# A sixth Strassen group in the input projection, and a branch's product moved into the attention loop

## The chip, the cores and the metric

The kernel runs on one core of one Trainium2 chip. A core has a matrix engine (TensorE, "PE" in the profile; its weight loads are shown as "PEld"), a vector engine (VectorE, "DVE"), an engine for activations and copies (ScalarE, "ACT"), a general engine (GpSimd, "POOL") and a queue engine (SyncE, "SP"). Each engine works through its own list of instructions in order, and waits for the others by semaphores. SP and POOL also issue the transfers between the chip's memory (DRAM) and the on-chip buffers. [...] The metric is the device time of one execution in microseconds (us); less is better.

## The reference

One layer of an encoder trunk over 1024 tokens of width 1024, in 32-bit numbers:

```python
h = x + 1/2 * SwiGLU_1(RMSNorm(x))
u = RMSNorm(h)
[qA|kA|vA|qB|kB|vB|gA|gB] = u @ W_in
yA = NeighbourhoodAttention2D(qA, kA, vA)       # 8 heads of 64, learned 2-D bias
yB = WindowedGQA(rope(qB), rope(kB), vB)        # 8 heads of 64 over 2 key heads, sink logit per head
h = h + (sigmoid(gA) * (yA @ W_A) + sigmoid(gB) * (yB @ W_B)) @ W_out
h = h + 1/2 * SwiGLU_2(RMSNorm(h))              # inner width 2816
y = RMSNorm_final(h)
```

W_in has 512 columns each for qA, kA, vA and qB, 128 each for kB and vB, and 1024 each for the gates gA and gB: 34 chunks of 128 columns, of which chunks 18 to 25 are gA and 26 to 33 are gB.

## The kernel before

Precision: every 32-bit factor is split into a high part (a cast on ACT) and the rest (a subtraction, mostly on DVE), and a product is made of three matmuls, high x high, high x low, low x high (mm3, lines 142 to 149). A plain product of one 128-column chunk with all 1024 tokens takes 8 blocks of the inner width x 2 halves of the tokens x 3 matmuls of 128x512.

Strassen: the two feed-forward stages, most of W_in and W_out are done in Strassen's scheme with seven products in place of eight. For W_in the list "groups" (line 875) names the chunks: a group is two pairs of chunks, and is worked as 7 products x 2 pairs x 4 blocks x 3 matmuls. The results are recombined as they leave PSUM (store_z, from line 879) and stored to DRAM: the first part of attention A's operands as high and low parts, the rest as z_d, and gate chunks to g_d. Chunks which are in no group are the list "gates" (line 877).

The attention loop (lines 1338 to 1362) then runs over 64 units: 32 of branch B (units_b, line 1223) and 32 of branch A (units_a, line 1242). A unit is one tile of 128 tokens and two heads. In iteration n the loop issues

- scores of unit n (line 1268): four matmuls into two PSUM banks of tag "d", on DVE the sum with the bias and the row's minimum, on ACT the exponential with its sum, on DVE the reciprocal, and the scaling of the two heads, one on DVE (line 1290) and one on ACT (line 1291);
- half of the iteration's share of filler steps;
- turn of unit n-1 (line 1293): up to six transposes into two more "d" banks, each split into high and low part by ACT and DVE;
- the other half of the filler;
- values of unit n-2 (line 1306) into a bank of tag "g", and the unit's write, which adds high and low parts on DVE.

There are four banks of tag "d" and four of tag "g". Branch B's write collects four units for a store to y_d, branch A's writes go to a part of the tile fa and are stored to y_d by halves; both stores are issued by POOL. Operands of attention A are fetched ahead by prep_a (line 1077). The bias of a head pair is fetched and added to the mask by load_bias when its first unit is made.

The filler (line 1199) is a generator of short pieces of matrix work, six matmuls a step: first the gates, eight steps a chunk, with the next chunk's weights loaded and split in between; then branch_b (line 1182), which multiplies branch B's attention output with W_B, four steps for each of eight chunks, applies the gate as the bank is read, and leaves the result in the tiles "merged"; at last six steps of branch A's product with W_A. How many filler steps an iteration takes is set by "rate" (line 1322); what is left is drained after the loop (line 1363). The gate's sigmoid is applied on ACT to the gate that is fetched back from g_d (gate_b, line 1176; a_prep, line 1390).

After the loop come the last W_B steps, the product with W_A (lines 1406 to 1424), whose operand is split from y_d by split_y, the merge with W_out (Down, line 1387), and the second feed-forward stage.

The order of instructions on each engine is the program's order as a planner sees it: the framework ranks the instructions by their place in the program, plays the engines through with assumed costs, takes the next one that is ready, and assigns free buffers and banks as it goes. Buffers are named by tags: raw (4), xs (2), ws (8), hs (6).

Of the kernel before, what the change touches and what calls it, by code (L numbers as in the profile page):

```python
# [15 lines left out]
P = 128  # L16
# [6 lines left out]
HD = 64  # L23
# [13 lines left out]
def trunk_kernel(ctx, tc, x, xt, n1, wg1, wu1, wd1, nm, win, rpb, sink, wa, wb, wo,  # L37
# [837 lines left out]
    groups = [[(12, 13), (14, 15)], [(16, 17), (0, 1)], [(4, 5), (8, 9)], [(2, 3), (6, 7)], [(10, 11), (18, 19)]]  # L875
# [192 lines left out]

    def load_bias(s, h):
        braw = raw4()[:, :384]  # L1070
        nc.sync.dma_start(braw, bias_d[h])
# [104 lines left out]
    def gate_b(dc):  # L1176
        rb = xs4()
        nc.sync.dma_start(rb, g_d[D + dc * P:D + (dc + 1) * P, :])
        nc.scalar.activation(rb, rb, AF.Sigmoid)
        return rb  # L1180

    def branch_b():

        for c in range(2, 4):
            split_y(Y_B[c], c * P, nc.vector if c == 2 else nc.gpsimd)
        for g in (4, 6):
            new_ar(g, F32)
        nxt = branch_w(wb[0], 0, nc.vector), gate_b(0)
        for dc in range(NC8):
            w, rb = nxt  # L1190
            bs = [bank("dg"[dc % 2]) for _ in range(2)]
            yield from branch_mm(bs, w, Y_B)
            if dc + 1 < NC8:
                nxt = branch_w(wb[0], dc + 1, nc.vector), gate_b(dc + 1)
            for n in range(2):
                sl = slice(n * 512, (n + 1) * 512)
                nc.vector.tensor_tensor(merged(dc)[:, sl], bs[n], rb[:, sl], op=ALU.mult)

    def filler():
        for dc, nxt in zip(gates, gates[1:] + [None]):  # L1200
            if nxt is not None:
                yield from gate(dc, {4: lambda: mix.update(gate=load_w(win[0], GA + nxt * P))})
            else:
                yield from gate(dc, {0: lambda: [fetch_y(c * P) for c in range(2)],
                                     4: lambda: [split_y(Y_B[c], c * P, nc.gpsimd) for c in range(2)],
# [12 lines left out]
    def small(name, n=2):  # L1218
        return main.tile([P, 2], F32, tag=name, bufs=n, name=nm_(name))

    ybox = {}

    def units_b():
        for j in range(NTT):
            for c in range(4):
                def write(o, j=j, c=c):

                    if c == 0:
                        ybox["b"] = xs4()[:, :512].rearrange("p (c t) -> p c t", c=4)
# [12 lines left out]
    def units_a():  # L1242
        for hp in range(4):
# [3 lines left out]
            for j in range(NTT):  # L1247
                def write(o, j=j, hp=hp):

                    y = fa[:, 3072:4096]  # L1250
# [3 lines left out]
                    for s in range(2):  # L1254
                        rows = slice(s * HD, s * HD + HD)
                        nc.vector.tensor_tensor(y[rows, j * P:(j + 1) * P], o[:HD, s, 0, :], lo[:, s, :], op=ALU.add)
                    if j in (3, 7) and hp < 3:
                        cols = slice((j - 3) * P, (j + 1) * P)
                        nc.gpsimd.dma_start(y_d[512 + hp * P:512 + (hp + 1) * P, cols], y[:, cols])
# [8 lines left out]
    def scores(un):  # L1268
# [7 lines left out]
        for s in range(2):  # L1276
# [3 lines left out]
            pr = fa[:, 1536 + (2 * (npair[0] % 2) + s) * (384 + ext):][:, :ext + nw]  # L1280
            if ext:
                nc.vector.tensor_copy(pr[:, 0:1], un["sink"][s])
# [8 lines left out]
        nc.scalar.activation(un["pr"][1], un["pr"][1], AF.Copy, scale=rc[:, 1:2])  # L1291
# [30 lines left out]
    rate = (nfill - 44) / 64.0  # L1322
# [15 lines left out]
    for n in range(1 << 30):  # L1338
# [218 lines left out]
```

## Time and profile before

| | |
|---|---|
| median of 3 runs | 1935.32 us (1935.28 to 1936.85) |
| profiled execution: span from the first to the last instruction | 1934.8 us; the page gives no other time of that execution |
| mean granted TensorE clock | 0.998 of full |
| TensorE busy | 1922.2 us, 99% |
| VectorE busy | 1437.1 us, 74% |
| ScalarE busy | 943.6 us, 49% |
| GpSimd busy | 295.5 us, 15% |
| projection W_in: first and last result copied from a bank by ACT (line 911) | 647.7 to 842.7 us of the span |
| attention loop (first and last score matmul) | 841.7 to 1114.7 us |
| branch B's product (its gate multiplications) | 1132.8 to 1169.4 us |
| branch A's gate multiplications | 1179.5 to 1212.9 us |

How to read the views. The page begins with each engine's busy time and its number of instructions; then the span is cut in 40 slices, with one digit of busy share, in tenths, for each. The chain of work that ended last is followed back from the last instruction and summed by engine and line. A row of groups reads: line, engine, operation, output<-inputs by the program's names, shapes, xcount | busy us, mean ns of one | idle time of the engine just before them, and what ended it. A row of the table by stretches reads: from:to, then time (length), and for PE, PEld, DVE, ACT and POOL the busy us and the number of instructions, the granted clock, the share of the transfer engines and GB/s. A row of the timeline reads: start us, length us, engine, line, operation. Matmuls are pipelined, so lengths of neighbours overlap; the distance of their starts tells their price.

### The profile page before, as it was taken

The page shows a single profiled execution, that of the slowest core. Times are in us where ns is not written, and L with a number is a line of the kernel's source. Part 1 is how long each engine was busy: PE and PEld are TensorE (multiplying, and loading weights), DVE is VectorE, ACT ScalarE, POOL GpSimd, SP SyncE. Part 2 cuts the span into 40 slices and gives each one's busy share as a digit, 9 for nine tenths or more (in the row PEclk, how much of TensorE's full clock was granted, in tenths as well). Part 3 has the DMA queues.
Part 4 walks back from the last instruction along what each step waited for, and adds up shares of the span by engine and source line. Part 5 has one row for each costly group of instructions (what it writes and reads, how often), then busy time and mean ns, then how long its engine had stood idle before and what let it go on. Part 6 is the DMA issues. An engine that isn't in the chain of part 4 may idle for free.

```text
span 1934.8 us, 25499 instructions
## 1 busy us (share of the span) xinstructions
PE 1922.2 (99%) x8956; PEld 1603.1 (83%) x8956; DVE 1437.1 (74%) x2560; ACT 943.6 (49%) x1827; POOL 295.5 (15%) x432
## 2 busy tenths in 40 slices
PE   9999999999999999999999999999999999999998
PEld 7888888888888888888888888878888888888886
DVE  7987765668957788678888857889676566569864
ACT  6532333344446543477877862365333333344453
POOL 0011110013300112211122231010111001005210
PEclk9999999999999999999999999999999999999999
DMA  6344323286234478553458576533423323493341
GB/s 261 100 167 163 129 104 128 86 289 225 88 109 137 159 223 250 185 163 104 116 134 195 184 242 210 169 140 133 147 87 109 126 87 109 140 355 104 112 144 61
DMA packets 151745, 298.70 MB, mean 154 GB/s; under 512 B 14912, under 2 KB 64448, under 8 KB 151616
## 3 DMA queue, kind: packets, MB, share of 16 engines
q1 hardware_dynamic: 123072, 210.53, 33.6%
q0 software_dynamic: 27824, 85.48, 13.3%
q8 instruction: 71, 1.16, 0.3%
q10 hardware_dynamic: 720, 1.05, 0.1%
q14 instruction: 58, 0.48, 0.1%
HBM read 210.50 MB, written 88.27 MB: 154 GB/s over the span
## 4 chain that ended last, share of the span: by engine, by line
PE 88%; issue 7%; POOL 1%; DMA 1%; DVE 1%; ACT 1%; POOLq 0%; SPq 0%; ACTq 0%; DVEq 0%
PE g L149 16%; PE g L147 16%; PE g L145 16%; PE d L149 11%; PE d L147 11%; PE d L145 11%; PE d L1299 2%; PE g L1313 1%; PE g L1318 1%; PE d L1278 1%; PE d L1279 1%; POOL zs_d L889 1%; PE d L138 1%; POOL z_d L891 1%; DMA zr_d<-xs 0%
## 5 line engine op out<-in xcount | busy, mean ns | idle before, releaser
L145 PE MATMUL g<-ar,ws 128*128 128x512 f32 x1128 | 423.1, 395 | 0.6 <-ACT fa L911 0.6
L147 PE MATMUL g<-ar,ws 128*128 128x512 f32 x1128 | 417.2, 390 | 0.9 <-DVE ar L94 0.5
L149 PE MATMUL g<-ar,ws 128*128 128x512 f32 x1128 | 416.1, 390 | 0.2 <-DVE ws L311 0.2
L145 PE MATMUL d<-ar,ws 128*128 128x512 f32 x736 | 282.4, 391 | 0.3 <-ACT ar L810 0.2
L147 PE MATMUL d<-ar,ws 128*128 128x512 f32 x736 | 281.9, 390 | 0.3 <-DVE ar L812 0.3
L149 PE MATMUL d<-ar,ws 128*128 128x512 f32 x736 | 281.6, 390 | 0.5 <-DVE ws L311 0.5
L147 PEld LDWEIGHTS g<-ar,ws 128*128 128x128 f32 x1128 | 211.8, 188 | 46.2 <-DVE ar L94 1.0
L149 PEld LDWEIGHTS g<-ar,ws 128*128 128x128 f32 x1128 | 211.7, 188 | 45.5 <-DVE ws L311 0.7
L145 PEld LDWEIGHTS g<-ar,ws 128*128 128x128 f32 x1128 | 206.4, 188 | 37.8 <-ACT fa L911 1.0
L311 DVE TENSOR_TENSOR ws<-raw,ws 128x512 fp32r<-128x512 f32 x204 | 139.6, 690 | 99.6 <-ACT ws L308 98.8
L308 ACT CAST ws<-raw 128x512 fp32r<-128x512 f32 x204 | 125.1, 620 | 140.6 <-PE g L149 64.4
L145 PEld LDWEIGHTS d<-ar,ws 128*128 128x128 f32 x736 | 138.3, 188 | 29.7 <-ACT ar L810 0.6
L147 PEld LDWEIGHTS d<-ar,ws 128*128 128x128 f32 x736 | 138.4, 188 | 29.6 <-DVE ar L812 0.6
L149 PEld LDWEIGHTS d<-ar,ws 128*128 128x128 f32 x736 | 138.4, 188 | 29.4 <-DVE ws L311 0.7
L93 ACT CAST ws<-raw 128x512 fp32r<-128x512 f32 (+1 forms) x121 | 81.0, 669 | 144.0 <-PE d L149 61.8
L94 DVE TENSOR_TENSOR ws<-raw,ws 128x512 fp32r<-128x512 f32 (+1 forms) x119 | 93.7, 789 | 59.8 <-ACT ws L93 59.3
L414 POOL DMA_DIRECT2D hid<-fx x91 | 49.3, 542 | 431.5 <-DVE fx L474 304.9
L93 ACT CAST ar<-raw 128x512 fp32r<-128x512 f32 (+1 forms) x83 | 56.0, 679 | 94.8 <-PE g L147 55.0
L94 DVE TENSOR_TENSOR ws<-ar,ws 128x512 fp32r<-128x512 f32 x114 | 98.3, 867 | 3.8 <-ACT ws L93 3.7
L145 PE MATMUL g<-ws,ws 128*128 128x512 f32 x232 | 91.0, 392 | 0.0
L149 PE MATMUL g<-ws,ws 128*128 128x512 f32 x232 | 90.5, 390 | 0.0
L147 PE MATMUL g<-ws,ws 128*128 128x512 f32 x232 | 90.3, 389 | 0.0
(313 smaller groups left out, 3607.4 us busy)
## 6 DMA issues: line engine op xcount, KB each, us to landing
raw<-hid SPq DMA_DIRECT2D x70, 512.0 KB
hid<-fx POOLq DMA_DIRECT2D x91, 256.0 KB, 2.4
ar<-in_ffn_w_down_dram SPq DMA_DIRECT2D x32, 512.0 KB
raw<-in_ffn_w_up_dram SPq DMA_DIRECT2D x31, 512.0 KB
raw<-in_ffn_w_gate_dram SPq DMA_DIRECT2D x27, 512.0 KB
raw<-in_w_in_dram SPq DMA_DIRECT2D x27, 512.0 KB
hid<-fa POOLq DMA_DIRECT2D x51, 256.0 KB, 2.7
ar<-zs_d POOLq DMA_DIRECT2D x48, 256.0 KB, 5.3
```

The lines of the kernel that those rows point to most:

```text
L93: nc.scalar.copy(dst_hi, src)
L94: (eng or nc.vector).tensor_tensor(dst_lo, src, f32v(dst_hi), op=ALU.subtract)
L138: nc.tensor.transpose(pt[:, c * P:(c + 1) * P], xs[:, (half * 4 + c) * P:(half * 4 + c + 1) * P], ident)
L145: nc.tensor.matmul(b, lhs[0], r[0], start=first, stop=False, **kw)
L147: nc.tensor.matmul(b, lhs[0], r[1], start=False, stop=False, **kw)
L149: nc.tensor.matmul(b, lhs[1], r[0], start=False, stop=last, **kw)
L308: nc.scalar.copy(w[0][:, :512], a)
L311: nc.vector.tensor_tensor(w[0][:, 512:], a, f32v(w[0][:, :512]), op=ALU.subtract)
L414: nc.gpsimd.dma_start(hid[PRODUCTS.index(p), i], src)
L889: nc.gpsimd.dma_start(d[ch * P:(ch + 1) * P, cols], t)
L891: nc.gpsimd.dma_start(z_d[ch * P:(ch + 1) * P, cols], c)
L1299: nc.tensor.transpose(pt[:, i * P:(i + 1) * P], un["pr"][s][:, i * P:(i + 1) * P], ident)
```

## The change

- A sixth group is added, chunks 20 to 23, which are four gate chunks of gA. The list "gates" gets shorter by them, from 14 to 10 chunks.
- The filler's rate is (nfill - 17) / 67 in place of (nfill - 44) / 64, so that most of branch_b's steps fall into the attention loop.
- sigmoid(g) is written as (1 + tanh(g/2)) / 2: ACT computes the tanh, the 1 is added where the gate multiplies the bank (scalar_tensor_tensor), and the half goes into the scale of the W_out merge (1.0 becomes 0.5).
- Attention is one unit deeper: turn works on unit n-2 and values on unit n-3; the scores have three buffers in place of two, and the small statistics three.
- The second head's scaling goes from ACT to POOL, the sink column's copy from DVE to POOL, the low half of a gate chunk's weight split from DVE to POOL. The splits of y, of which POOL had six, are all on DVE.
- The writes of a unit are one DVE operation of 64x256 in place of two of 64x128, except for the last head pair, whose y is split in two halves as it comes.
- The stores of y go to the list "stores" and are issued by SP in the next iteration, in smaller pieces.
- Biases are fetched by fetch_bias in iterations 29, 37, 45 and 53; gates two chunks ahead (fetch_gate). Biases, branch weights and y use the tag hs.

```diff
-    groups = [[(12, 13), (14, 15)], [(16, 17), (0, 1)], [(4, 5), (8, 9)], [(2, 3), (6, 7)], [(10, 11), (18, 19)]]
+    groups = [[(12, 13), (14, 15)], [(16, 17), (0, 1)], [(4, 5), (8, 9)], [(2, 3), (6, 7)], [(10, 11), (18, 19)], [(20, 21), (22, 23)]]
...
+    def hs4():
+        return main.tile([P, 512], F32, tag="hs", bufs=6, name=nm_("hs"))
+
+    def fetch_bias(hp):
+        mix["bias", hp] = [hs4()[:, :384] for _ in range(2)]
+        for s in range(2):
+            nc.sync.dma_start(mix["bias", hp][s], bias_d[2 * hp + s])
+
     def load_bias(s, h):
-        braw = raw4()[:, :384]
-        nc.sync.dma_start(braw, bias_d[h])
+        braw = mix["bias", h // 2][s]
...
-            r = fetch_branch(raw4()[:, :512], w, dc)
+            r = fetch_branch(hs4(), w, dc)
...
-    def gate_b(dc):
-        rb = xs4()
-        nc.sync.dma_start(rb, g_d[D + dc * P:D + (dc + 1) * P, :])
-        nc.scalar.activation(rb, rb, AF.Sigmoid)
-        return rb
+    def fetch_gate(dc):
+        mix["rb", dc] = xs4() if dc % 3 else raw4()
+        nc.sync.dma_start(mix["rb", dc], g_d[D + dc * P:D + (dc + 1) * P, :])
+
+    def open_gate(dc):
+        nc.scalar.activation(mix["rb", dc], mix["rb", dc], AF.Tanh, scale=0.5)
 
     def branch_b():
 
         for c in range(2, 4):
-            split_y(Y_B[c], c * P, nc.vector if c == 2 else nc.gpsimd)
+            split_y(Y_B[c], c * P, nc.vector)
         for g in (4, 6):
             new_ar(g, F32)
-        nxt = branch_w(wb[0], 0, nc.vector), gate_b(0)
+        fetch_gate(1)
+        w = branch_w(wb[0], 0)
+        open_gate(0)
         for dc in range(NC8):
-            w, rb = nxt
             bs = [bank("dg"[dc % 2]) for _ in range(2)]
-            yield from branch_mm(bs, w, Y_B)
-            if dc + 1 < NC8:
-                nxt = branch_w(wb[0], dc + 1, nc.vector), gate_b(dc + 1)
+            mm = branch_mm(bs, w, Y_B)
+            for c in range(4):
+                drain(mm, 1)
+                yield
+                if c == 0 and dc + 2 < NC8:
+                    fetch_gate(dc + 2)
+                if c == 1 and dc + 1 < NC8:
+                    w = branch_w(wb[0], dc + 1)
+                    open_gate(dc + 1)
+            rb = mix.pop(("rb", dc))
             for n in range(2):
                 sl = slice(n * 512, (n + 1) * 512)
-                nc.vector.tensor_tensor(merged(dc)[:, sl], bs[n], rb[:, sl], op=ALU.mult)
+                nc.vector.scalar_tensor_tensor(out=merged(dc)[:, sl], in0=rb[:, sl], scalar=1.0, in1=bs[n],
+                                               op0=ALU.add, op1=ALU.mult)
...
-                yield from gate(dc, {4: lambda: mix.update(gate=load_w(win[0], GA + nxt * P))})
+                yield from gate(dc, {4: lambda: mix.update(gate=load_w(win[0], GA + nxt * P, eng=nc.gpsimd))})
...
+                                     3: lambda: fetch_gate(0),
+                                     4: lambda: [split_y(Y_B[c], c * P, nc.vector) for c in range(2)],
...
-                    for s in range(2):
-                        nc.vector.tensor_tensor(ybox["b"][s * HD:s * HD + HD, c, :], o[:HD, s, :], lo[:, s, :], op=ALU.add)
-                    if c == 3:
-                        nc.gpsimd.dma_start(y_d[:512, j * P:(j + 1) * P].rearrange("(c p) t -> p c t", p=P), ybox["b"])
+                    nc.vector.tensor_tensor(ybox["b"][:, c % 2], o[:HD], lo, op=ALU.add)
+                    if c % 2:
+                        stores.append((y_d[(c - 1) * P:(c + 1) * P, j * P:(j + 1) * P].rearrange("(c s p) t -> p c s t", s=2, p=HD),
+                                       ybox["b"]))
...
-            pr = fa[:, 1536 + (2 * (npair[0] % 2) + s) * (384 + ext):][:, :ext + nw]
+            pr = fa[:, 1536 + (2 * (npair[0] % 3) + s) * (384 + ext):][:, :ext + nw]
             if ext:
-                nc.vector.tensor_copy(pr[:, 0:1], un["sink"][s])
+                nc.gpsimd.tensor_copy(pr[:, 0:1], un["sink"][s])
...
-        nc.scalar.activation(un["pr"][1], un["pr"][1], AF.Copy, scale=rc[:, 1:2])
+        nc.gpsimd.tensor_scalar(un["pr"][1], un["pr"][1], rc[:, 1:2], None, op0=ALU.mult)
...
-    rate = (nfill - 44) / 64.0
+    rate = (nfill - 17) / 67.0
...
-        if len(pipe) > 1 and pipe[1] is not None:
-            turn(pipe[1])
+        if len(pipe) > 2 and pipe[2] is not None:
+            turn(pipe[2])
         if prep:
             drain(prep, 1)
+        while stores:
+            nc.sync.dma_start(*stores.pop())
+        if n in (29, 37, 45, 53):
+            fetch_bias((n - 29) // 8)
...
         if n in (60, 61, 62):
-            split_y(Y_A[n - 60], 512 + (n - 60) * P, nc.gpsimd)
+            split_y(Y_A[n - 60], 512 + (n - 60) * P, nc.vector)
         filling(0.5)
-        if len(pipe) > 2 and pipe[2] is not None:
-            values(pipe[2])
-        pipe = pipe[:3]
+        if len(pipe) > 3 and pipe[3] is not None:
+            values(pipe[3])
+        pipe = pipe[:4]
...
-    down = Down(4, wo[0], 1.0, place, quarter, {k: left_d[i] for i, k in enumerate(("P5", "P6", "P3", "P7"))},
+    down = Down(4, wo[0], 0.5, place, quarter, {k: left_d[i] for i, k in enumerate(("P5", "P6", "P3", "P7"))},
```

More of the change, by code (lines that the diff above doesn't have):

```diff
@@ L1215, in trunk_kernel, with small @@
     nfill = len(gates) * 8 + 38
-    def small(name, n=2):
+    def small(name, n=3):
         return main.tile([P, 2], F32, tag=name, bufs=n, name=nm_(name))
-    ybox = {}
+    ybox, stores = {}, []
     def units_b():
@@ L1253, in write @@
                     nc.vector.tensor_tensor(lo, o[:HD, :, 1, :], lo, op=ALU.add)
[L1254 to L1259, printed above, removed]
+                    cols = slice(j % n * P, j % n * P + P)
+                    if hp == 3:
+                        for s in range(2):
+                            nc.vector.tensor_tensor(ybox["a"][s * HD:s * HD + HD, cols], o[:HD, s, 0, :], lo[:, s, :], op=ALU.add)
+                        if j % n == n - 1:
+                            cols = slice((j - n + 1) * P, (j + 1) * P)
+                            split(slot(22)[:, cols], slot(23)[:, cols], ybox["a"])
+                        return
+                    y = ybox["a"][:HD].rearrange("p (s t) -> p s t", s=2)
+                    nc.vector.tensor_tensor(y[:, :, cols], o[:HD, :, 0, :], lo, op=ALU.add)
+                    if j % n == n - 1:
+                        stores.append((y_d[512 + hp * P:512 + (hp + 1) * P, (j - n + 1) * P:(j + 1) * P]
+                                       .rearrange("(s p) t -> p s t", p=HD), y))
                 edge = 1 if j in (0, NTT - 1) else 0
@@ L1368, in trunk_kernel @@
         a_raw[i] = fetch_branch(t[:, (i - 2) // 2, i % 2 * 512:i % 2 * 512 + 512], wa[0], a_order[i])
-    split(slot(22), slot(23), fa[:, 3072:4096])
     for t in range(4):
@@ L1392, in a_prep @@
         nc.sync.dma_start(r, g_d[dc * P:(dc + 1) * P, :])
-        nc.scalar.activation(r, r, AF.Sigmoid)
+        nc.scalar.activation(r, r, AF.Tanh, scale=0.5)
         return r
```

11 lines of the change are left out of this document (6 added, 5 removed).

## The prediction

> **What bounds the kernel now.** First the page: busy shares, slices, chain.
>
> ```profile
> span 1934.8 us, 25499 instructions
> PE 1922.2 (99%) x8956; PEld 1603.1 (83%) x8956; DVE 1437.1 (74%) x2560; ACT 943.6 (49%) x1827; POOL 295.5 (15%) x432
> ...
> PE   9999999999999999999999999999999999999998
> ...
> DVE  7987765668957788678888857889676566569864
> ...
> PE 88%; issue 7%; POOL 1%; DMA 1%; DVE 1%; ACT 1%; POOLq 0%; SPq 0%; ACTq 0%; DVEq 0%
> ```
>
> TensorE works in every slice and holds 88% of the chain. The page gives no time beside the span; the median of the runs, 1935.32, is 0.5 us above it, and I add 0.5 at the end. Then busy time by stretch (time and count of PE, PEld, DVE, ACT, POOL): a dense stretch, all of attention, two pieces of attention, and what follows it.
>
> ```profile
> 320.00:560.00 240.00, 240.00 (x1060) 198.72 (x1060) 174.35 (x236) 97.75 (x171) 48.34 (x44) 1.00 0.48 165
> 840.00:1120.00 280.00, 279.33 (x1648) 245.17 (x1647) 236.08 (x773) 225.80 (x575) 54.74 (x82) 1.00 0.56 150
> 1000.00:1020.00 20.00, 20.00 (x124) 17.81 (x123) 18.85 (x61) 15.99 (x44) 7.33 (x14) 1.00 0.68 176
> 1055.00:1112.00 57.00, 57.00 (x338) 49.99 (x337) 50.42 (x158) 49.08 (x122) 11.82 (x11) 1.00 0.70 194
> 1120.00:1180.00 60.00, 60.00 (x270) 49.55 (x269) 24.39 (x41) 29.25 (x40) 14.14 (x11) 1.00 0.78 256
> ```
>
> Busy alone proves little for pipelined matmuls, so I read the spacing: 240/1060 = 0.2264 us for one 128x512 matmul in the dense stretch. Attention is as full: the matmul timeline of one unit there has no hole.
>
> ```profile
> 903.40 0.34 PE L1278 MATMUL d<-ar,ar 128*128 128x384 f32 x1
> ...
> 904.11 0.63 PE L145 MATMUL g<-ar,ws 128*128 128x512 f32 x2
> ...
> 905.50 0.82 PE L1299 MATMUL d<-ident,fa 128*128 128x128 f32 x6
> 906.07 0.96 PE L1318 MATMUL g<-ws,fx 128*128 128x256 f32 x6
> 906.87 0.34 PE L1278 MATMUL d<-ar,ar 128*128 128x384 f32 x1
> ```
>
> By starts: scores 0.71, one filler step (six matmuls) 1.39, transposes 0.57, values 0.80. A unit costs 2.08 us plus 1.39 per filler step. So whatever takes matmuls away shortens the run, as long as DVE, ACT, POOL and the banks keep this pace.
>
> **The change, part by part.** *Sixth group.* Four gate chunks leave the filler: each has 8 x 2 x 3 = 48 matmuls, 192 in all. A group has 7 products x 2 x 4 x 3 = 168. Saved: 24 x 0.2264 = 5.4 us. Its operands add weight splits and recombinations on DVE and ACT to a kind of work that is dense today; DVE has 174.35 of 240 there, so I charge nothing. Loads and gate stores only move from the filler.
>
> *Pace of attention.* Filler steps fall from 14 x 8 + 38 = 150 to 118, the rate from 106/64 = 1.656 to 101/67 = 1.507 a unit. A unit then takes 2.08 + 1.507 x 1.39 = 4.17 us. The gates end at step 80, iteration (80 - 3)/1.507 = 51; by iteration 63, 99.4 steps are used. So 19.4 steps of branch B now lie in the last 13 scoring iterations, and 18.6 steps remain, 18.6 x 6 x 0.2264 = 25 us.
>
> *DVE in these 13 iterations.* The prices, from the groups of 1055 to 1112 (13 units, as the reciprocals count) and of the whole run:
>
> ```profile
> L1256 DVE TENSOR_TENSOR fa<-g,s 64x128 f32<-64x128 f32 x26 | 7.3, 281 | 0.2
> L1253 DVE TENSOR_TENSOR s<-g,s 64x256 f32<-64x256 f32 x14 | 5.7, 410 | 0.4 <-ACT s L1252 0.3
> L94 DVE TENSOR_TENSOR ws<-raw,ws 128x1024 fp32r<-128x1024 f32 x3 | 3.7, 1219 | 0.6 <-ACT ws L93 0.6
> L1073 DVE TENSOR_TENSOR fa<-raw,masks 128x384 f32<-128x384 f32 x4 | 2.1, 552 | 0.1
> L1289 DVE RECIPROCAL rc<-ssum 128x2 f32<-128x2 f32 x13 | 2.1, 162 | 1.4 <-ACT fa L1286 1.2
> L94 DVE TENSOR_TENSOR fx<-d,fx 128x256 fp32r<-128x256 f32 x4 | 1.7, 423 | 0.0
> L1197 DVE TENSOR_TENSOR ar<-g,xs 128x512 f32<-128x512 f32 x8 | 5.2, 686 | 13.5 <-PE g L149 8.3 <-ACT raw L1393 4.2 <-ACT xs L1179 1.0
> L311 DVE TENSOR_TENSOR ws<-raw,ws 128x512 fp32r<-128x512 f32 x204 | 139.6, 690 | 99.6 <-ACT ws L308 98.8
> ```
>
> Attention itself: 50.42 - 3.7 - 2.1 - 1.7 = 42.9, or 3.30 a unit. One write of 0.410 for two of 0.281 saves 8 x 0.152 = 1.2: 41.7. Bias sums and V splits come back, 3.8. Branch B costs 0.690 + 2 x 0.686 = 2.06 a chunk, 4.85 chunks: 10.0. Five y splits, two of branch B and three of A, at 1.219: 6.1. Half a split for the last head: 0.7. Sum 62.3 us against 13 x 4.17 = 54.2: DVE is short by 8.1 us. Before iteration 51 it gains: the gate splits (1.219) and the sink copies leave it.
>
> What may cover the 8.1: the pipeline has one unit more, 4.17 us; 25 us of filler are left that the planner can put forward (in the old trace, too, filler steps stand split around transposes); behind them DVE has room, 24.39 of 60 today. And at 18.85 of 20 (1000 to 1020) PE lost nothing. PE's loss lies between 0 and 8.1; nearest is the row at 94% with no loss; I take 1.1.
>
> *Two banks fewer.* Even chunks of branch B hold two of the four d banks through their four steps, in which scores and transposes rotate: 12 steps in the loop, 12/1.507 = 8 units.
>
> ```profile
> 907.05 0.55 DVE L94 TENSOR_TENSOR ws<-d,ws 128x384 fp32r<-128x384 f32 x1
> ...
> 908.05 0.55 DVE L94 TENSOR_TENSOR ws<-d,ws 128x384 fp32r<-128x384 f32 x1
> ```
>
> These free the transposes' banks at 907.60 and 908.60; the next scores began at 906.87, their second pair at 907.22. With two banks they wait up to 1.38 us unless a filler step (1.39) lies between; at 0.75 steps a half, it lies there three times in four. That is 8 x 0.25 x 1.38 = 2.8 us, at most 11, at least 0. I take 0 in the sum, since the planner can place the step there, and keep 2.8 as a rival.
>
> *ACT and POOL.*
>
> ```profile
> L1291 ACT ACTIVATE fa<-fa,rc 128x384 f32<-128x384 f32 (+1 forms) x64 | 38.1, 595 | 2.8 <-DVE rc L1289 1.8 <-DVE fa L1282 0.9
> L1282 DVE COPY fa<-nsk 128x1 f32<-128x1 f32 x64 | 8.5, 142 | 4.6 <-DMA z_d<-fa 3.8 <-ACT fa L1286 0.5 <-DMA g_d<-fa 0.3
> L94 POOL TENSOR_TENSOR ws<-ar,ws 128x512 fp32r<-128x512 f32 x6 | 7.7, 1291 | 19.0 <-ACT ws L93 19.0
> L94 POOL TENSOR_TENSOR ar<-raw,ar 128x1024 fp32r<-128x1024 f32 x6 | 14.8, 2464 | 22.0 <-ACT ar L93 22.0
> L126 POOL TENSOR_SCALAR st<-st 128x1 f32<-128x1 f32 x20 | 7.6, 379 | 206.3 <-ACT xs L123 206.0
> L1179 ACT ACTIVATE xs<-xs 128x1024 f32<-128x1024 f32 x8 | 8.5, 1061 | 10.8 <-DMA xs<-g_d 10.7
> L1179 ACT ACT_TABLE_LOAD x1 | 1.3, 1283 | 0.0
> ```
>
> ACT loses 38.1 us of scaling, more than branch B's gates (8 x 1.061) bring in. POOL takes 64 scalings between 0.379 (one column) and 1.291 (two inputs, 512 columns): 24 to 83 us; 64 sink copies, about 24; nine gate splits, 9 x 2.464 = 22; it sheds six y splits, 15. At most 54.74 + 83 + 24 + 22 - 15 = 169 of some 270 us. Behind a scaling that waits for the sums stand the next unit's sink copies, which its exponential needs; the unit more of depth covers about 1 us of that. Next gate's weights have four steps, 4/1.507 x 4.17 = 11 us, for a load, a cast and 2.464. Price 0.
>
> If tanh and exp evicted each other's table, 4.85 chunks x 2 x 1.283 = 12.4 us would fall on ACT. No run here shows a tanh; I take 0, since 128 exponentials among copies cost one load. [...]
>
> POOL beside DVE has a price in the trace, in the stages where POOL subtracts:
>
> ```profile
> L94 DVE TENSOR_TENSOR ws<-ar,ws 128x512 fp32r<-128x512 f32 x114 | 98.3, 867 | 3.8 <-ACT ws L93 3.7
> L1290 DVE TENSOR_SCALAR fa<-fa,rc x64: 336/420/966, 850.0 to 1117.7; 128x384 f32<-128x384 f32 x48, 128x256 f32<-128x256 f32 x16
> ```
>
> 0.867 against 0.690: 0.18 us for an SBUF difference. Such operations among the 62.3 us are about 14: 2.5 us more. [...]
>
> *Stores, bias, tail.* Fourteen y stores leave POOL, 28 smaller ones go on SP, an iteration after their write; behind them wait weight and gate loads that are needed 11 us later. Bias loads go ahead by three units. All 0.
>
> Sum: 1934.8 - 5.4 + 1.1 = 1930.5, with the 0.5: 1931.0.
>
> **The rivals.** *Same: the two banks.* 2.8 us more of waiting: 1933.8. For it: bank release lies 1.4 us after the scores' start. Against: the scores and transposes can be moved around the filler.
>
> *Slower: DVE is the bound of iterations 51 to 63.* The 8.1 are not covered and the port adds 2.5: 1934.8 - 5.4 + 10.6 + 0.5 = 1940.5. It decides from 5.4 + 3.9 = 9.3 us of PE idle there. For it: the ledger. Against: 25 us of filler behind it.
>
> *The change doesn't do what it says:* tanh reloads tables, 12.4 us on ACT, which without its scalings and with the gates holds 49.08 - 13 x 0.595 + 4.85 x 1.061 = 46.5 of 54.2. So 4.7 to 12.4 of it show: 1934.6 to 1942.3.
>
> **How the numbers follow.** Forecast 0.50 (own range 1929.4 to 1931.4), two banks 0.20, DVE bound 0.25, tables 0.05 (half of it slower). A measurement tells 0.2%, 3.9 us, from no change. Faster 0.50, same 0.22, slower 0.28. The range goes from 1928.5 (a little waiting of today also goes: attention's 280 us hold 0.7 of PE idle) to 1942.
>
> **What would show it.** PE's instructions fall by about 24. Attention starts 168 x 0.2264 = 38 us later, lasts some 14 us less, and branch A follows it within some 25 us. Right: PE full from 840 to the merge, DVE over 90% in the last 55 us of attention. Wrong: PE idle there, released by DVE or a d bank; weight loads waiting for POOL's gate splits; more than four table loads; the exponential waiting for POOL's sink copy.

## The result, and the profile after

Before 1935.33 us (median of 5 runs, 1935.28 to 1936.85), after 1943.37 us (5 runs, 1942.32 to 1943.70): ratio 1.0037, 95% interval 1.0026 to 1.0047. The changed kernel is slower by 8.0 us between the medians (7.2 by the ratio), where 1931.0 was forecast; the time lies 1.4 us above the top of the range.

The page of the changed kernel, the same parts as before:

```profile
span 1941.9 us, 25728 instructions
PE 1921.7 (99%) x8932; PEld 1601.1 (82%) x8932; DVE 1435.4 (74%) x2462; ACT 914.8 (47%) x1773; POOL 389.4 (20%) x553
...
PE   9999999999999999999999999999999999999998
...
DVE  7987765668957788557778887889666566559864
...
PE 84%; issue 9%; DMA 2%; DVE 2%; POOL 2%; ACT 1%; POOLq 0%; SPq 0%; ACTq 0%; DVEq 0%
```

The 24 matmuls are gone (8956 to 8932 records), and TensorE is busy 0.5 us less while the span is 7.1 us longer. The slices show nothing, a slice being 48.5 us. So I made one ledger for all kernels from the matmul records: to each matmul its normal spacing (0.2265 us with 512 columns, 0.174 with 384, 0.12 with 256, 0.11 with 128), and what lies between two starts beyond that counts as waiting. "Attention" goes from the first scores to the last values. In us:

| kernel | matmul work before, in, after attention | waiting before, in, after | first scores, last values at |
|---|---|---|---|
| before | 830.9, 278.6, 797.9 | 8.8, 5.3, 4.5 | 841.9, 1124.9 |
| after | 868.9, 266.3, 766.6 | 9.2, 18.0, 3.9 | 880.4, 1163.8 |

Work fell by 5.6 us in all; waiting in attention rose by 12.7; the rest is within 0.6. These sums explain 6.9 of the 7.1 us of span. The windows (time and count of PE, PEld, DVE, ACT, POOL; granted clock; DMA share; GB/s) give the place:

```profile
880.00:1080.00 200.00, 199.07 (x1185) 175.51 (x1184) 157.41 (x470) 143.87 (x379) 123.18 (x170) 1.00 0.53 145
1080.00:1160.00 80.00, 72.53 (x409) 61.73 (x407) 71.24 (x195) 58.36 (x140) 24.01 (x24) 0.96 0.68 205
...
1088.00:1094.00 6.00, 4.41 (x31) 3.89 (x29) 5.11 (x17) 5.93 (x17) 2.97 (x5) 1.00 1.22 326
1094.80:1098.20 3.40, 3.12 (x9) 2.74 (x10) 3.10 (x7) 1.95 (x4) 0.76 (x2) 0.50 1.11 323
1146.00:1149.40 3.40, 3.40 (x16) 3.02 (x15) 3.35 (x9) 2.63 (x6) 0.34 (x1) 0.50 0.21 65
```

The first 200 us lose 0.93 us. The last 80, in which branch B joins (its first matmuls start at 1095.46), lose 7.5 us of busy time, and hold two stretches of 3.4 us in which the granted clock is 0.50 and the matmuls with 512 columns stand about 0.43 us apart, against 0.2265: some 1.7 us lost in each, which the busy column doesn't show. DVE is at 71.24 of 80, 89%. The waits there are many and small (waiting engine and line, what it waits for: us, times, longest):

```profile
POOL fa L1318 <- DVE rc L1316: 44.2, 13, 7.3
ACT fa L1313 <- DVE nmx L1310: 9.3, 6, 1.9
...
PE g L1340 <- DVE ws L94: 2.1, 2, 1.8
...
PE d L145 <- DVE ws L94: 1.9, 1, 1.9
```

One of the largest in the timeline (start, us, engine, operation; in brackets the idle time and its releaser):

```profile
1091.76 1.21 DVE L94 TENSOR_TENSOR ar<-raw,ar 128x1024 fp32r<-128x1024 f32 x1
...
1092.68 0.63 ACT L1313 ACTIVATE fa<-fa,nmx 128x384 f32<-128x384 f32 x1
...
1093.43 0.17 DVE L1316 RECIPROCAL rc<-ssum 128x2 f32<-128x2 f32 x1 [0.46 <-ACT fa L1313]
1093.52 0.54 DVE L94 TENSOR_TENSOR ws<-d,ws 128x384 fp32r<-128x384 f32 x1
...
1094.20 0.59 PE L1340 MATMUL g<-ws,fx 128*128 128x256 f32 x3 [1.79 <-DVE ws L94]
...
1095.34 1.06 ACT L1188 ACTIVATE xs<-xs 128x1024 f32<-128x1024 f32 x1
...
1098.53 0.08 DVE L1310 DVE_READ_ACCUMULATOR2_ANT nmx<- 128x1 f32 x1
...
1099.76 1.06 ACT L1188 ACTIVATE raw<-raw 128x1024 f32<-128x1024 f32 x1 [0.96 <-DMA raw<-g_d]
...
1100.73 0.60 ACT L1313 ACTIVATE fa<-fa,nmx 128x384 f32<-128x384 f32 x1
```

The transposed attention weights had to be split on DVE before TensorE could go on, and it waited 1.79 us. DVE was in a y split until 1092.97; then it stood idle for 0.46 us, because the reciprocal that came next in its order waited for an exponential on ACT; only after that did it split the weights. Some us later the same happens on ACT: the next exponential has its minimum from DVE at 1098.61, but starts at 1100.73, since a copy and a tanh stand before it, the tanh at a load that has not landed.

### The profile page after: what moved, and what is told of

It reads as the page before. It is cut to its first block, busy times and chain, and to the rows that moved or that the text cites. A ratio compares the mean times of both kernels' runs of the same rounds, so it can differ in the third digit from the quotient of the medians.

```text
span 1941.9 us, 25728 instructions
## 1 busy us (share of the span) xinstructions
PE 1921.7 (99%) x8932; PEld 1601.1 (82%) x8932; DVE 1435.4 (74%) x2462; ACT 914.8 (47%) x1773; POOL 389.4 (20%) x553
## 3 DMA queue, kind: packets, MB, share of 16 engines
q10 hardware_dynamic: 720, 1.05, 0.1%
## 4 chain that ended last, share of the span: by engine, by line
PE 84%; issue 9%; DMA 2%; DVE 2%; POOL 2%; ACT 1%; POOLq 0%; SPq 0%; ACTq 0%; DVEq 0%
PE g L149 15%; PE g L145 15%; PE g L147 15%; PE d L145 11%; PE d L149 11%; PE d L147 11%; PE d L1326 2%; PE g L1345 1%; PE g L1340 1%; PE d L1305 1%; PE d L1306 1%; POOL zs_d L889 1%; DMA g_d<-fa 1%; POOL z_d L891 1%; PE d L138 1%
## 5 line engine op out<-in xcount | busy, mean ns | idle before, releaser
L145 PE MATMUL g<-ar,ws 128*128 128x512 f32 x1096 | 414.0, 394 | 1.1 <-ACT ws L93 0.9
L147 PE MATMUL g<-ar,ws 128*128 128x512 f32 x1096 | 409.2, 390 | 0.4 <-DVE ar L833 0.4
L149 PE MATMUL g<-ar,ws 128*128 128x512 f32 x1096 | 408.8, 390 | 0.3 <-DVE ws L311 0.3
L145 PE MATMUL d<-ar,ws 128*128 128x512 f32 x760 | 293.7, 392 | 2.2 <-DVE ws L94 1.9
L147 PE MATMUL d<-ar,ws 128*128 128x512 f32 x760 | 293.0, 392 | 0.6 <-DVE ar L812 0.6
L149 PE MATMUL d<-ar,ws 128*128 128x512 f32 x760 | 292.4, 391 | 0.5 <-DVE ws L311 0.5
L149 PEld LDWEIGHTS g<-ar,ws 128*128 128x128 f32 x1096 | 205.7, 188 | 44.3 <-DVE ws L311 0.7
L147 PEld LDWEIGHTS g<-ar,ws 128*128 128x128 f32 x1096 | 205.6, 188 | 43.7 <-DVE ar L833 0.8
L145 PEld LDWEIGHTS g<-ar,ws 128*128 128x128 f32 x1096 | 201.2, 188 | 38.0 <-ACT ws L93 1.3
L311 DVE TENSOR_TENSOR ws<-raw,ws 128x512 fp32r<-128x512 f32 x210 | 143.6, 689 | 107.3 <-ACT ws L308 106.4
L145 PEld LDWEIGHTS d<-ar,ws 128*128 128x128 f32 x760 | 143.0, 189 | 32.3 <-issue 2.2
L147 PEld LDWEIGHTS d<-ar,ws 128*128 128x128 f32 x760 | 143.1, 188 | 30.6 <-DVE ar L812 1.2
L149 PEld LDWEIGHTS d<-ar,ws 128*128 128x128 f32 x760 | 143.0, 188 | 30.4 <-DVE ws L311 1.1
L93 ACT CAST ws<-raw 128x512 fp32r<-128x512 f32 (+1 forms) x107 | 70.6, 660 | 143.0 <-PE d L149 61.0
L94 DVE TENSOR_TENSOR ws<-raw,ws 128x512 fp32r<-128x512 f32 x98 | 72.2, 737 | 56.4 <-ACT ws L93 56.4
L1318 POOL TENSOR_SCALAR fa<-fa,rc 128x384 f32<-128x384 f32 (+1 forms) x64 | 82.4, 1288 | 84.7 <-DVE rc L1316 59.1
L1313 ACT ACTIVATE fa<-fa,nmx 128x385 f32<-128x385 f32 (+3 forms) x128 | 75.6, 591 | 36.5 <-DVE nmx L1310 33.0
L145 PE MATMUL g<-ws,ws 128*128 128x512 f32 x232 | 91.0, 392 | 0.0
```

The costliest lines, as they stand in the source:

```text
L93: nc.scalar.copy(dst_hi, src)
L94: (eng or nc.vector).tensor_tensor(dst_lo, src, f32v(dst_hi), op=ALU.subtract)
L145: nc.tensor.matmul(b, lhs[0], r[0], start=first, stop=False, **kw)
L147: nc.tensor.matmul(b, lhs[0], r[1], start=False, stop=False, **kw)
L149: nc.tensor.matmul(b, lhs[1], r[0], start=False, stop=last, **kw)
L311: nc.vector.tensor_tensor(w[0][:, 512:], a, f32v(w[0][:, :512]), op=ALU.subtract)
```

## The experiments

Each is timed beside the kernel before on the same chip. Waiting is the ledger's figure for attention in the profiled execution; after has 18.0, before 5.3. The last column counts the windows of 3.413 us in attention in which the granted clock was 0.50; each adds up to 1.7 us to the waiting. After has two, before none.

| run | median us | ratio to before, 95% interval | waiting | windows at 0.50 |
|---|---|---|---|---|
| e1_gbanks | 1946.07 | 1.0051, 1.0034 to 1.0068 | 19.0 | 1 |
| e2_late | 1942.27 | 1.0034, 1.0022 to 1.0046 | 15.5 | 0 |
| e3_group_only | 1946.51 | 1.0050, 1.0035 to 1.0065 | 18.8 | 0 |
| e4_ysplit_pool | 1953.62 | 1.0088, 1.0073 to 1.0103 | 26.3 | 3 |
| e5_scale_act | 1949.48 | 1.0065, 1.0049 to 1.0082 | 25.3 | 3 |
| e6_rest_only | 1937.53 | 1.0005, 0.9996 to 1.0014 | 5.2 | 0 |
| e7_no_ylo | 1944.17 | 1.0038, 1.0023 to 1.0053 | 18.8 | 2 |
| e8_level | 1945.23 | 1.0044, 1.0029 to 1.0059 | 19.5 | 1 |
| e9_no_gate_load | 1939.56 | 1.0018, 1.0008 to 1.0027 | 14.6 | 0 |
| e10_tied_tanh | 1947.88 | 1.0063, 1.0048 to 1.0078 | 22.9 | 3 |
| e11_tied_14 | 1941.64 | 1.0031, 1.0019 to 1.0042 | 16.4 | 0 |
| e12_pad | 1957.39 | 1.0112, 1.0097 to 1.0127 | 12.8 | 1 |
| e13_tanh_copy | 1942.81 | 1.0036, 1.0024 to 1.0047 | 17.8 | 1 |
| e14_tanh_copy_level | 1937.39 | 1.0007, 0.9998 to 1.0017 | 12.4 | 0 |
| e15_late_casts | 1938.04 | 1.0009, 1.0000 to 1.0018 | 13.1 | 0 |

**The rivals of the prediction: banks, and DVE's share.**

```
e1  -            bs = [bank("dg"[dc % 2]) for _ in range(2)]
    +            bs = [bank("g") for _ in range(2)]
```

> The changed kernel with every chunk of branch B's product in two g banks (before: d and g in turn), so that scores and transposes keep all four d banks. Banks theory (scores and transposes wait because even chunks hold two of four d banks): in the changed kernel's trace some 5.3 us of PE gaps end at d banks and one of the two drops to half clock (1.7 us) follows such a gap, so about 7 us go: 1936. Vector theory (VectorE has more work in the last 13 units than TensorE): nothing is taken from VectorE, so 1942 to 1944.

Waiting 19.0: leaving scores and transposes all four d banks takes nothing off it. (Branch B then holds two of the four g banks throughout; the run doesn't price that by itself.)

```
e2  -    rate = (nfill - 17) / 67.0
    +    rate = (nfill - 44) / 64.0
```

> The changed kernel with the old filler rate formula (nfill - 44) / 64, which is 1.156 steps a unit: the gates last until iteration 66 and branch B's product lies behind the loop, as in the kernel before. A unit then takes 2.08 + 1.156 x 1.39 = 3.69 us of TensorE. Banks theory and vector theory alike: no chunk of branch B meets scores any more and VectorE needs some 3.2 of 3.69 us, so the loss goes and the 5.4 us saved show: 1930 to 1931. Rival (the loop at this pace is bound by ScalarE, VectorE or GpSimd): over 1935.

Branch B is out of the loop, the end of attention is no longer crowded, and 15.5 us of waiting are still there, now at the start, around 1075 and at the end. So the place follows the filler, the amount hardly does. Both theories had the loss gone here; neither holds as it was put.

```
e4  six of the seven split_y, three of branch B and three of branch A: nc.vector -> nc.gpsimd
```

> The changed kernel with the six splits of y back on GpSimd as in the kernel before. Vector theory: 6 x 1.22 = 7.3 us less VectorE work in iterations 49 to 62, so the loss there falls by about 6 us: 1937. Banks theory: 1942 to 1944.

Work taken off DVE gave the worst time of the runs that add no matmuls: on GpSimd a y split takes 2.47 us in this run, against 1.22 on DVE, and TensorE waits 2.3 us for one. Nor is DVE relieved where it counts:

```profile
1090.34 5.30 DVE L1317 TENSOR_SCALAR fa<-fa,rc 128x384 f32<-128x384 f32 x1
1090.68 4.74 POOL L94 TENSOR_TENSOR ar<-raw,ar 128x1024 fp32r<-128x1024 f32 x2
...
1096.04 1.54 PE L1326 MATMUL d<-ident,fa 128*128 128x128 f32 x6 [3.33 <-DVE ws L94]
```

Beside two y splits on GpSimd (second line) a scaling on DVE, which takes 0.42 us in the median, lasts 5.30, and TensorE waits 3.33 us for the weight split behind it. So this run is no clean test of DVE's share.

**Which part of the change.**

```
e3  before.py, only:  groups = [..., [(10, 11), (18, 19)], [(20, 21), (22, 23)]]
e6  after.py without that sixth group, rate = (nfill - 44) / 64.0 as before
```

> The kernel before with the sixth group alone and nothing else of the change (rate (118 - 44) / 64 = 1.156, a unit 3.69 us of TensorE). VectorE needs 3.30 a unit in attention A, some 0.25 for the gate splits, and V splits and bias sums beside; so 3.7 to 3.8. Vector theory: attention becomes bound by VectorE, the loss is about 64 x 0.1 = 6 us or more against the 5.4 saved: 1935 to 1940. If the planner hides that: 1930.

> The changed kernel without its sixth group, at the filler rate of before (1.656 steps a unit, branch B after the loop): the other parts of the change alone. Ledger and cover theory: the sixth group's missing filler is what hurts, so attention's waits are 4 to 6 us as before and the time is 1933 to 1936. Lock theory: the POOL scalings hurt here as well, waits over 9 us, 1939 to 1943.

The one row of each, over attention, says it:

```profile
880.00:1120.00 240.00, 231.22 (x1405) 199.57 (x1404) 220.87 (x744) 206.18 (x541) 47.88 (x75) 1.00 0.57 150
```

```profile
840.00:1120.00 280.00, 279.14 (x1650) 246.56 (x1649) 212.72 (x647) 197.61 (x510) 158.92 (x202) 1.00 0.56 153
```

With the sixth group alone (first row) TensorE loses 8.8 of 240 us; with everything but the group (second) 0.9 of 280, as before, though DVE is relieved from 236.08 to 212.72 and GpSimd carries the scaling. All that is lost comes with the group, most likely with the 32 filler steps that attention no longer has (on which more below); the rest of the change by itself neither helps nor harms (within 0.14%), and beside the group it gives back less than a third of the loss (1.0050 to 1.0037, intervals that overlap).

```
e5  -        nc.gpsimd.tensor_scalar(un["pr"][1], un["pr"][1], rc[:, 1:2], None, op0=ALU.mult)
    +        nc.scalar.activation(un["pr"][1], un["pr"][1], AF.Copy, scale=rc[:, 1:2])
```

> The changed kernel with the scaling of the second head on ACT again, as in the kernel before; all else as changed. Lock theory (64 POOL scalings of 1.288 us stand in the chain of a unit and hold up DVE's SBUF operations beside them): attention's waits of TensorE fall from 18.0 us to below 10, 1934 to 1937 us. Ledger theory (DVE has too much to do from iteration 49 on): at most 2 us better, 1941 to 1944. Cover theory (with 38 us less of filler in attention, whatever stands in the way of a unit shows, on ACT too, which gets some 38 us back): 1943 to 1948.

Worse by 1.0065 against 1.0037, some 5 us: the scaling is better off on GpSimd, whatever it does to DVE. Its profiled execution (1953.2) is the slowest of its four; of the 25.3 us, 5.5 stand in one place, on which more below.

**Is it DVE's work?**

```
e7  split_y: the cast as before, then DVE only on the first 1 (branch A) or 16 (branch B) columns;
    the low part of all other y is left out
e8  rate = 1.4 if n < 56 else 2.9
```

> The changed kernel with the DVE half of the six y splits cut to a sliver (16 columns or 1 instead of 1024 elements a row), so branch A and branch B lack the low part of these y rows: work is left out. It takes 6 x 1.2 = 7.2 us off DVE between iterations 49 and 63 and puts it nowhere. Ledger theory: TensorE's waits in attention fall by 5 to 7 us, 1936 to 1939. Lock and cover theory: they fall by 3 us at most, 1940.5 to 1943.

> The changed kernel with the same steps in the same sequence, but spread otherwise: 1.4 filler steps a unit up to iteration 55 (the gates), 2.9 from there on (branch B), so that 25 us of filler that came after the loop lie beside the last units. By row 880 to 1080 of the changed kernel DVE then has some 3.4 us per unit of 4.0 us, and 5.7 per 6.1 at the end. Ledger theory: attention's waits fall from 18.0 to 6 to 10 us, 1932 to 1936. Cover theory: waits move but stay above 13, 1938 to 1944. Lock theory: unchanged, 1942 to 1944.

Neither moved the time. With 6.5 us less on DVE (1428.9 against 1435.4) the waiting stayed at 18.8, with one wait of 6.5 us while DVE stood idle for 7.6. The ledger theory falls as it stood in the prediction: a sum of DVE work against the length of a stretch. DVE is not cleared by this, though: from 1110 to 1160 TensorE is busy for 47.79 us in this run, 45.83 in the changed kernel, and the one long wait takes that back. This wait shows something else:

```profile
1099.72 0.40 PE L145 MATMUL d<-ar,ws 128*128 128x512 f32 x1
...
1102.78 1.06 ACT L1190 ACTIVATE xs<-xs 128x1024 f32<-128x1024 f32 x1 [4.95 <-DMA xs<-g_d]
...
1103.74 0.60 ACT L1315 ACTIVATE fa<-fa,nmx 128x384 f32<-128x384 f32 x1
...
1105.06 0.17 DVE L1318 RECIPROCAL rc<-ssum 128x2 f32<-128x2 f32 x1 [7.62 <-ACT fa L1315]
...
1106.63 0.87 PE L1328 MATMUL d<-ident,fa 128*128 128x128 f32 x3 [6.51 <-DVE ws L94]
...
1127.43 1.27 DVE L1215 SCALAR_TENSOR_TENSOR ar<-xs,g 128x512 f32<-128x512 f32 x2
```

A tanh of branch B (line 1190 there) waits 4.95 us on ACT for its gate load. Its result isn't needed before the gate multiplication at 1127.43, but the exponential of the next unit stands behind it, then the reciprocal, then the transposes. With the scaling on ACT it is a y load in the place of the gate load:

```profile
1095.21 1.04 ACT L93 CAST ar<-raw 128x1024 fp32r<-128x1024 f32 x1 [6.55 <-DMA raw<-y_d]
...
1098.14 0.69 PE L1305 MATMUL d<-ar 128*128 128x384 f32 x1 [5.52 <-DVE nmx L1310]
```

Both stand where the last pair of heads is loaded (iteration 49 to 51, twelve loads of 256 KB); the DMA share there is 1.22 and 1.11 in the changed kernel's rows for 1088 to 1098. The program calls a chunk's tanh half a chunk before that chunk begins (open_gate(dc + 1)), and the planner, which takes what its assumed costs call ready, can put it earlier still: in the changed kernel the tanh of chunk 1 (xs, 1095.34) stands ahead of that of chunk 0 (raw, 1099.76).

**Loads that ACT stands at.** In the changed kernel, 880 to 1180 (the longest, 3.8 us, ends at 1175.4, behind attention's last values at 1163.8):

```profile
ACT raw L1423 <- DMA raw<-g_d: 5.5, 2, 3.8
...
ACT xs L1188 <- DMA xs<-g_d: 3.5, 2, 2.1
...
ACT raw L1188 <- DMA raw<-g_d: 1.1, 2, 1.0
```

```
e9   fetch_gate and a_prep without their loads; the tanh reads masks[:, :1024], the gates' values are left out
e10  open_gate(dc) in dc's own chunk, its scale from a tile: half = rc * 0 + 0.5 on GpSimd,
     rc the reciprocals of the latest unit
e11  e10 with rate = 1.4
```

> The changed kernel without the sixteen gate loads of branch B and branch A: the tanh reads the mask tile instead, so the gates' values are left out, the tanh itself stays. In the changed kernel ACT waits in attention 10.1 us for these loads (5.5 at the tanh of branch A, 4.6 at that of branch B), and the exponentials behind it in ACT's order wait with it. Head-of-line theory (a tanh that waits for its load holds up the units' exponentials): TensorE's waits in attention fall from 18.0 us to 9 to 13, 1935 to 1939 us. Cover theory (with the filler gone the units' latency shows whatever ACT does): 16 to 19, 1941 to 1944.

> The changed kernel with each tanh tied to its time: its scale of 0.5 is read from a small tile that GpSimd makes from the reciprocals of the latest unit, so that it cannot stand in ACT's order about a chunk before it is needed; everything is computed, at 16 small GpSimd instructions more. Head-of-line theory: the loads have landed by then, ACT waits for gate loads under 3 us, TensorE's waits in attention fall to 9 to 13 us, 1935 to 1939. If the tanh now comes too late for the banks: TensorE waits for the gate product, 1943 to 1948. Cover theory: 1941 to 1944.

> The tied tanh again, and 1.4 filler steps a unit all through, so that the gates end at iteration 55 and branch B starts after the loads of the last pair of heads (issued at iteration 49 to 51), and 24 steps are left behind the loop. If those loads were what made the gate and y loads late: better than the tied tanh alone by 2 us or more, 1932 to 1936. If it is the thinner cover (1.4 steps a unit) that counts: worse than it by 2 us or more.

Without the loads 3.4 us of waiting go, less than head-of-line had asked for (9 to 13 left; 14.6 are) and more than cover; in time it is 1.0018 against 1.0037, 3.7 us. The run has no window at half clock where the changed kernel has two, and these alone are some 3.4 us; TensorE's idle time from 880 to 1160 falls by 1.3 only, from 8.4 to 7.1 us. It also takes sixteen loads of 512 KB off the memory, and does not separate that traffic from ACT's standing at them. Tying the tanh did not bring this: ACT's waits for gate loads fell to 2.0 us, but the waiting rose to 22.9, with two waits of 2 to 3 us at other places. With branch B starting at 55 instead of 51 the same kernel gains 6 us (1.0031 against 1.0063); that fits the loads of the last pair as what makes the others late, but the run also leaves 25 steps behind the last scores in place of 19, and does not separate the two.

```
e13  gate(): nc.scalar.copy(gt, bs[n]) -> nc.scalar.activation(gt, bs[n], AF.Tanh, scale=0.5);
     no tanh in branch_b, nor in a_prep for chunks 6 and 7; the other six tied to the last unit
e14  e13 with rate = 1.4 if n < 56 else 2.9
```

> The changed kernel with the tanh of ten gate chunks taken where they are copied out of their banks, so that branch B's gates come back from memory finished and ACT waits for none of their loads; the tanh of the other six (branch A) is tied to the last unit. All is computed; ACT loses 10 x 1.06 us. Head-of-line theory, as the run without gate loads put it (3.8 us): TensorE's waits in attention fall from 18.0 to 12 to 15 us, 1937.5 to 1941. If fewer waits of ACT only uncover the next one: 16 to 19, 1941 to 1944.

> The same with the filler spread as 1.4 steps a unit to iteration 55 and 2.9 after it. If the levelled run gained nothing only because its gate loads came late (4.2 us of its 19.5 stand behind them): waits in attention 8 to 13 us, 1933 to 1938, better than the run before it by 2 us or more. Cover theory: what levelling gives at the end it takes from the gates' part; 14 to 18, within 2 us of the run before it.

The tanh at the copy alone gives nothing (1.0036), the levelled filler alone gave nothing (1.0044), together they give 1.0007: 5.8 us better than the changed kernel, with 12.4 us of waiting and no window at half clock, which is 3.4 of the 5.6 us of waiting that went. (The profiled execution, 1936.44 us, lies 0.95 below the median of its ten.) Removing one wait only uncovers the next as long as several crowd in one place. What is left is again of this kind:

```profile
1135.35 1.05 ACT L93 CAST ar<-raw 128x1024 fp32r<-128x1024 f32 x1 [2.43 <-DMA raw<-y_d]
...
1138.10 0.73 PE L145 MATMUL d<-ar,ws 128*128 128x512 f32 x2 [1.63 <-ACT ws L93]
```

```
e15  e14; prep_a loads V first; branch A's three y casts tied to the units 62 to 64
```

> The levelled run with the tanh taken at the copy, and two more loads given more time: prep_a issues V's load ahead of its other loads (TensorE waited 1.9 us for its transposes at 1051), and the three casts of branch A's y on ACT are tied to the reciprocals of iterations 62 to 64 instead of standing in ACT's order from iteration 60 on (ACT waited 6.1 us for their loads, TensorE 1.8 us at 1136). All is computed. Head-of-line theory: TensorE's waits in attention fall from 12.4 to 8 to 10 us, 1933.0 to 1935.5, level with the kernel before or a little better. Cover theory: others take their place, 12 to 14 us, 1936.5 to 1939.

The wait at 1136 went, two of 1.4 and 1.75 us at weight casts came at 1112 and 1162, and the 1.9 us at V's transposes stayed. No version here beats the kernel before.

**Is it the cover?**

```
e12  +        if got is not None and n >= 49:
     +            b = bank("g")
     +            for i in range(6):
     +                nc.tensor.matmul(b, got["q"][0], got["kd"][0][:, :512], start=i == 0, stop=i == 5)
```

> The changed kernel with work added that is of no use: in each of the iterations 49 to 63 six more 128x512 matmuls into a bank that nobody reads, 15 x 6 x 0.2264 = 20.4 us of TensorE. Cover theory (the units' chains through ACT and DVE take longer than the thinner filler lasts): the added work goes into the waits, which fall from 18.0 us in attention to 6 to 10, and the run gets longer by 9 to 13 us only, 1952 to 1956. If the waits have causes that do not depend on the pace (a late store, a lock, a fixed delay): they stay near 18, and the run gets longer by 18 to 21, 1961 to 1964.

The useless work of 20.4 us lengthens the run by 0.0075, 14.5 us, between the two expectations: waiting falls from 18.0 to 12.8. The window tells why it isn't more:

```profile
1110.00:1160.00 50.00, 50.00 (x279) 43.38 (x279) 40.50 (x112) 31.22 (x74) 13.51 (x9) 1.00 0.38 127
```

From 1110 to 1160 TensorE loses nothing at all, with DVE at 81%; the changed kernel, in the same 50 us, loses 4.2:

```profile
1110.00:1160.00 50.00, 45.83 (x264) 39.01 (x262) 45.97 (x130) 36.59 (x87) 12.37 (x11) 0.97 0.51 166
```

What is left stands at 1094 and 1104, where branch B begins and ACT still waits 4.7 us for gate loads, and at 1161. So in these 50 us the loss is the thin cover; at branch B's start it is not that alone.

The first 200 us of attention, with gates as their only filler, say the same without added work. In order: everything but the group (1.656 filler steps a unit), the levelled run (1.4) and the late run (1.156); the changed kernel, at 1.507, has its row above.

```profile
842.00:1042.00 200.00, 199.82 (x1180) 176.68 (x1179) 145.27 (x449) 139.71 (x366) 120.47 (x164) 1.00 0.54 142
```

```profile
880.00:1080.00 200.00, 196.69 (x1185) 173.89 (x1184) 154.51 (x479) 142.28 (x381) 123.73 (x172) 1.00 0.55 144
```

```profile
880.00:1080.00 200.00, 193.61 (x1191) 171.21 (x1190) 166.38 (x521) 149.43 (x410) 132.20 (x180) 1.00 0.59 153
```

TensorE idles 0.2 us at 1.656 steps, 0.9 at 1.507, 3.3 at 1.4 and 6.4 at 1.156, with DVE at 73 to 83%, below the 94% at which the prediction saw no loss: the thinner the filler, the more of the units' chains shows. The wait at attention's start is one such: DVE stands there for the projection's last stores out of the tile fa, 4.1 us in all in the kernel before, where TensorE doesn't wait for it, and 5.8 us in the late run, where it waits 2.3.

## Why the prediction was wrong

- **Sixth group, -5.4 us: right.** 24 matmul records fewer, 5.6 us less matmul work. Attention starts 38.5 us later, as said.
- **Pace of attention and PE's loss, +1.1 us: the step that failed.** Attention was to last some 14 us less; it lasts 283.4 us after 283.0. In place of 1.1 the term is 12.7, of which 3.4 are two windows at half clock, each right behind a wait of about 2 us (1.94 and 2.04). The bounds I gave it, 0 to 8.1, came from the DVE ledger alone. I took the low end by the row at 94% without a loss, which stands where nothing but attention and gates ran, and named as cover a deeper pipeline and 25 us of filler behind the loop. Neither covered it: the filler behind the loop, pulled in (levelled run), changed nothing by itself. What the step left out is that the filler steps are the cover: each unit has a chain through ACT, DVE and GpSimd, and with 1.4 or 1.156 steps a unit TensorE loses 3.3 and 6.4 us of 200 while no engine is full.
- **Rival "DVE is the bound": the sign was right and its 1940.5 comes near, but its cause is not borne out.** DVE stood at 89% in 1080 to 1160; 6.5 us less on it changed nothing in the sum. The 2.5 us that its sum puts down to a port are an estimate from two rows, 0.867 against 0.690 us; no run shows a port. What the runs show in its place are single long scalings on DVE beside subtractions on GpSimd, up to 2.16 us in the changed kernel and 5.30 in the run with the y splits on GpSimd. What the sum misses is order: ACT and DVE work through a list, and an item that waits for a load holds up the unit behind it.
- **ACT and loads, price 0: wrong.** I compared 46.5 us of ACT work with 54.2 and said that weight and gate loads are needed 11 us later. They are needed then, but ACT stands at them before that. Without the gate loads the run is 3.7 us shorter, the half-clock windows included.
- **Rival "two banks", 2.8 us: not borne out.** With four d banks free the waiting was 19.0; nothing speaks against the price 0.
- **Rival "tables": out.** The changed kernel loads three tables, one of them in attention, where the kernel before loads four; at the lines of the tanh, 1188 and 1423, there is none:

```profile
L740 ACT ACT_TABLE_LOAD x1 | 1.3, 1283 | 1.2 <-PEq L1559 1.2
...
L1313 ACT ACT_TABLE_LOAD x1 | 1.3, 1283 | 0.0
...
L470 ACT ACT_TABLE_LOAD x1 | 1.3, 1283 | 0.0
```

- **GpSimd, price 0: borne out with the full filler.** The 64 scalings take 82.4 us, at the upper end of my 24 to 83; one of 128x384 takes more than the 1.291 us that I had as its bound (first row: 1.368). DVE's own scaling, of 0.422 us in the median, reaches 2.158 (second row):

```profile
L1318 POOL TENSOR_SCALAR fa<-fa,rc 128x384 f32<-128x384 f32 x48 | 65.7, 1368 | 61.6 <-DVE rc L1316 37.9 <-PE d L1306 5.9 <-PE g L1340 5.5
```

```profile
L1317 DVE TENSOR_SCALAR fa<-fa,rc x64: 333/422/2158, 886.7 to 1156.5; 128x384 f32<-128x384 f32 x48, 128x256 f32<-128x256 f32 x16
```

  The four longest, 1.05 to 2.16 us, each end within 0.3 us of the end of a GpSimd subtraction of 2.4 us, the split of a gate's weights, not beside a GpSimd scaling. Whether the one held up the other is not shown; in the run of all but the group, with the full filler, nothing of it shows in the time (1.0005). With the thin filler such a long scaling can cost: the one of 5.30 us in the run with the y splits on GpSimd stands ahead of a wait of 3.33 us. The scalings on GpSimd are no loss even there, since undoing them costs some 5 us. No weight load waited for a gate split, and the exponential waited for GpSimd 1.2 us once.

Shown, then: the loss comes with the group; it grows as the filler beside a unit gets thinner, and moves with it; from 1110 to 1160 added matmuls remove it; without the gate loads 3.7 us go. Two windows at half clock (3.4 us) belong to the 12.7, but no run removes them alone. Not shown is whether the gate loads cost by ACT standing at them or by their traffic. Open stays what keeps the best of these versions at 12.4 us of waiting against 5.3, that is, what besides the thin filler makes the waits at V's transposes and at branch B's first weights.

## What to carry to other kernels

Matmuls that fill a latency-bound loop are cover: taking 32 steps out of it to save 24 matmuls elsewhere cost more than twice the saving, and the price is to be read from the chain that the filler hides, not from the share of the busiest engine. On an engine that works in order, look for operations that wait for a load ahead of the critical ones; doing such an operation earlier, where its data is at hand (the tanh at the copy), removes the wait, but shows only once the other waits of that stretch are spread as well. Where several small waits crowd together, undo or cure them in pairs before you call one innocent.

## What the runs showed of the hardware

The granted clock fell to 0.50 for 3.413 us right behind waits of about 2 us (1.94 and 2.04 us of waiting, at 1092 and 1143, drops at 1094.8 and 1146.0). The length of a single wait doesn't decide it: the levelled run shows a drop after a wait of 2.1 us and none after one of 2.4, and the late run none after 2.5. Where the wait lies fits better. The two drops stand 51.20 us apart, 15 times 3.413, and the trace of the changed kernel has one more of that length at the span's start (16.20), 316 such windows ahead of the first. Of the windows laid from these drops, from 25 to 1900 us and by the modelled ends of the matmuls, the two that a drop follows hold 1.81 and 1.87 us without a matmul (the first and the second row), and no other more than 0.97:

```profile
1091.40:1094.81 3.41, 1.60 (x12) 1.23 (x10) 2.95 (x7) 3.39 (x10) 1.71 (x2) 1.00 1.37 236
1142.60:1146.01 3.41, 1.54 (x8) 1.07 (x7) 3.41 (x11) 1.67 (x5) 1.24 (x1) 1.00 0.45 154
```

In the kernel before, by windows laid from its drop at 15.98, none there holds more than 0.80, and none is followed by a drop. In the levelled run the wait of 2.1 us lies within one window of its grid (1080.67 to 1084.08, 1.89 us without a matmul), the wait of 2.4 across the line at 1118.22. No run moves a wait across such a line by itself, so this is a reading of these traces. Each drop of the changed kernel cost some 1.7 us on top of its wait.
